# Rounding and subtracting two heads of queries and keys at once, with transfers inside SBUF, in the setups of a decoder layer's two attentions

## The chip, the core and the metric

The kernel runs on one core of a Trainium2 chip. The core has a matrix engine (TensorE, PE in the profile; its weight loads are PEld), a vector engine (VectorE, DVE), a scalar engine (ScalarE, ACT), a general engine (GpSimd, POOL) and a sync engine (SyncE, SP) that issues transfers. Every engine works through its own instructions in the order in which they were built; semaphores make one wait for another. Data lives in SBUF (128 partitions) and in PSUM, which TensorE writes; transfers between HBM and SBUF, or from one place in SBUF to another, run on 16 DMA engines that all queues share. The metric is device time in microseconds from start to end of one execution.

## What is computed

One layer of a hybrid decoder, for a prompt of 1024 tokens and for 8 single-token samples with 8192 cached tokens each. The parts that matter here are the prompt's forgetting attention, 8 heads of 64 columns:

```
def mixer_inputs(xn, w_in, b_f, g_sgu_v):
    h = xn @ w_in
    q = h[..., O_Q:O_K].reshape(B, T, ATT_HEADS, ATT_HEAD_DIM)
    k = h[..., O_K:O_V].reshape(B, T, ATT_HEADS, ATT_HEAD_DIM)
    ...
def fox_attend(q, k, v, cq, ck, qpos, kpos):
    s = einsum('bqhd,bkhd->bhqk', q, k) * ATT_HEAD_DIM ** -0.5
    s = s + (cq[..., :, None] - ck[..., None, :])
    s = where(kpos <= qpos, s, -inf)
    p = softmax(s, axis=-1)
    return einsum('bhqk,bkhd->bqhd', p, v)
```

Around it stand the input projection, a spatial gating unit, an output projection, a cross-attention into 256 memory tokens, a gated MLP with a causal convolution, and for the samples the same layer with attention over a paged cache of keys and values. All inputs and outputs are float32.

## The kernel before

Matrix products of the prompt are made in three parts from operands that are split in two: a high part h, the value rounded to the matrix format fp32r, and a low part l, the value minus h. The prompt runs in one order of stages: input projection, first attention (rows 0 to 511, `hf` 0), second attention (rows 512 to 1023, `hf` 1), then output projection, cross-attention and MLP for each half. The sample work (gathers of cached keys and values, VectorE multiplications and reductions over keys, lines 1427 and 1428 in the attentions, TensorE products over values, line 1488) is laid between at a rate that is set by hand for each stage. The order on each engine is fixed when the kernel is built, by a list scheduler with its own picture of durations; SP and GpSimd issue their transfers in that order too, and an issue that waits holds up what stands behind it.

An attention runs over four head pairs (`hp`), each of two heads (`j`), two blocks of queries (`blk`) and two query tiles (`ii`). Each score tile is two products: the operand `qq[:, 0]` with `ka`, and `qq[0:68, 1]` with `kb` (lines 807 and 809). By partitions:

- `qq[0:64, 0]` and `qq[0:64, 1]` both hold the head's high queries, `qq[64:128, 0]` its low queries, `qq[64:68, 1]` four rows of cumulated gates;
- `ka[0:64]` and `ka[64:128]` both hold the high keys, `kb[0:64]` the low keys, `kb[64:68]` four more gate rows.

So high by high and low by high come from the first product (contracted over 128 partitions), high by low and the gates from the second (over 68).

`setup(hp)` makes these operands in two steps. `load` has fetched the two heads' queries `qn` (one buffer), keys `kn` and values `vn` with tokens on partitions. Step one transposes the queries on TensorE into one PSUM tile `tr` (line 750), whose partitions 0 to 63 are head 0 and 64 to 127 head 1. Then, for each head, ScalarE rounds 64 partitions into `qq[0:64, 0]` (757), GpSimd copies them to `qq[0:64, 1]` (758), and VectorE subtracts into `qq[64:128, 0]` (774). Step two does the same for the keys (transposes 779; 784, 785, 788). In the first attention the prepared keys are stored to `ks_d` (791, 792), and in the second one loaded from there for the first 512 tokens (769, 770). `calm` orders ScalarE's part behind the newest exponential.

The setup of the next head pair is started while the present one is half done: step one after the first block, step two one score tile later. The very first setup is called early, at the end of the input projection, ahead of that projection's last group of matmuls; the second attention's first setup begins in the first attention's last head pair. Between a setup and its first score stand the current pair's last scores, exponentials (813 to 817), transposes of probabilities ("turns", 836, evacuated by 841 and 843) and value products (852, 861, 872). During the first attention, matmuls that prepare the cross-attention's memory (lines 272 to 274, loads of `w_ck` and `w_cv` on SP by line 249) and the spatial gating (631 to 679) are laid between. During the second attention PSUM's four single banks of the pool `ba` become two pairs, so that a score tile of up to 1024 columns has one pair, and the setups' `tr` takes half a pair.

Of the pools, `U` has 18 tiles of 4 KB a partition, `T2` has 7 of 2 KB, the raw weights `wr` 4, and the gathered cache rows `kv` 4. Each is used in turn, and a tile is waited for until what it held has been read.

Of the kernel before, what the change touches and what calls it, by code (L numbers as in the profile page):

```python
# [7 lines left out]
F32 = mybir.dt.float32  # L8
F32R = mybir.dt.float32r
BF16 = mybir.dt.bfloat16  # L10
I32 = mybir.dt.int32
AF = mybir.ActivationFunctionType
ALU = mybir.AluOpType
# [65 lines left out]
def build(nc, tc, ctx, a, phases=None):  # L79
# [27 lines left out]
    def nm(s):  # L107
        cnt[0] += 1
        return f"{s}_{cnt[0]}"

    def U(shape, dt=F32):
        n = 1
        for s in shape[1:]:
            n *= s
        t = upool.tile([P, UW], dt, tag="u", bufs=NU, name=nm("u"))[:, :n]
        if len(shape) == 3:
            t = t.rearrange("p (a b) -> p a b", b=shape[2])
        return t

    def T2(n=512, dt=F32):  # L120
        return tpool.tile([P, 512], dt, tag="t2", bufs=NT, name=nm("t2"))[:, :n]
# [88 lines left out]
    ks_d = dram.tile([NH, 64, 2, 512], F32, tag="ks_d", name="ks_d")  # L210
# [515 lines left out]
    def attention(hf, late=None, at=3):  # L726
# [3 lines left out]
        def load(hp):  # L730
# [9 lines left out]
            nc.sync.dma_start(vn, v_d[: nk * P, cs].rearrange("(i p) c -> p i c", p=P))  # L740
            return qn, kn, vn

        def setup(hp, qn, kn, vn):


            calm = lambda: tc.issue_after(lastexp[0]) if lastexp else nullcontext()
            with behind(ENG.PE):
                tr = (MS, BB, BA)[SB]()
                for i in range(4):
                    nc.tensor.transpose(tr[:, i * P : (i + 1) * P], qn[:, i, :], ident)  # L750
            qab, ka, kb = [], [], []
            for j in range(2):
                h = hp * 2 + j
                rows = slice(64 * j, 64 * j + 64)
                qq = U([P, 2, 512], F32R)
                with calm():
                    nc.scalar.activation(qq[0:64, 0, :], tr[rows, :], AF.Copy)
                nc.gpsimd.tensor_copy(qq[0:64, 1, :], qq[0:64, 0, :].bitcast(F32))
                nc.gpsimd.dma_start(qq[64:68, 1, :], cq_d[h, :, hf * 512 : (hf + 1) * 512])
                qab.append(qq)  # L760
                if hf == 0:
                    kab = U([P, 2, 512], F32R)
                    ka.append(kab[:, 0, :])
                    kb.append(kab[:, 1, :])
                else:
                    ka.append(U([P, nk * P], F32R))
                    kb.append(U([P, nk * P], F32R))
                    for r in range(2):
                        nc.sync.dma_start(ka[j][64 * r : 64 * r + 64, 0:512].bitcast(F32), ks_d[h, :, 0, :])
                    nc.sync.dma_start(kb[j][0:64, 0:512].bitcast(F32), ks_d[h, :, 1, :])  # L770
                nc.gpsimd.dma_start(kb[j][64:68, :], ck_d[h, :, : nk * P])
            for j, qq in enumerate(qab):
                rows = slice(64 * j, 64 * j + 64)
                nc.vector.tensor_tensor(qq[64:128, 0, :], tr[rows, :], qq[0:64, 0, :].bitcast(F32), op=ALU.subtract)
            yield
            with behind(ENG.PE):
                tr = (MS, BB, BA)[SB]()
                for i in range(4):
                    nc.tensor.transpose(tr[:, i * P : (i + 1) * P], kn[:, i, :], ident)
            s = slice(hf * 512, hf * 512 + 512)  # L780
            for j in range(2):
                rows = slice(64 * j, 64 * j + 64)
                with calm():
                    nc.scalar.activation(ka[j][0:64, s], tr[rows, :], AF.Copy)
                nc.gpsimd.tensor_copy(ka[j][64:128, s], ka[j][0:64, s].bitcast(F32))
            for j in range(2):
                rows = slice(64 * j, 64 * j + 64)
                nc.vector.tensor_tensor(kb[j][0:64, s], tr[rows, :], ka[j][0:64, s].bitcast(F32), op=ALU.subtract)
            if hf == 0:
                for j in range(2):  # L790
                    nc.gpsimd.dma_start(ks_d[hp * 2 + j, :, 0, :], ka[j][0:64, :].bitcast(F32))
                    nc.gpsimd.dma_start(ks_d[hp * 2 + j, :, 1, :], kb[j][0:64, :].bitcast(F32))
            got.append((qab, ka, kb, vn))

        def scores(qkv, ls, blk, j, ii):
# [90 lines left out]

        got = []
        first = setup(0, *load(0))
        if hf:
            next(first)  # L890
# [5 lines left out]
        for hp in range(4):  # L896
# [5 lines left out]
            for blk in range(2):  # L902
# [6 lines left out]
                for j in range(2):  # L909
                    for ii in range(2):  # L910
                        p_ = scores(qkv, ls, blk, j, ii)
                        if ii == 0:
                            pt.append(
                                [
                                    (U([P, 4, 256]) if nkt - g > 2 else T2(512).rearrange("p (a b) -> p a b", b=256))
                                    for g in range(0, nkt, 4)
                                ]
                            )
                        queue.append(partial(turn, p_, pt[j], nkt - 1 + ii, ii))
                        if j == 1 and ii == 1:  # L920

                            def fin(*args):
                                r = values(*args)
                                queue.insert(min(BKQ, len(queue)), partial(back, *r))

                            queue.append(partial(fin, qkv, ls, pt, hp, blk))
                        drain(LA[hf])
                        yield 1.8
                        if hp < 3 and (blk, j, ii) == LD[hf]:
                            raw = load(hp + 1)  # L930
                        if hp < 3 and (blk, j, ii) == ST[hf]:
                            nxt = setup(hp + 1, *raw)
                        if nxt:
                            next(nxt, None)
                            yield 1
# [425 lines left out]
    def behind(e):  # L1361

        return tc.issue_after(last[e]) if e in last else nullcontext()
# [480 lines left out]
    def prompt():  # L1844
# [4 lines left out]

        got, ahead = [], []  # L1850
        att1 = attention(1, lambda: got.append(merge_in(0)))
        att0, fill0 = attention(0, (lambda: next(att1)) if LT < 4 else None, LT), fill()

        def early():
# [170 lines left out]
```

## Time and profile before

| what | us |
|---|---|
| runs of the kernel before | 1807.2, 1799.28, 1805.22; median 1805.22 |
| the profiled execution's own time | 1804.14 |
| its span, first to last instruction | 1802.1 |

A profile's group line reads: source line, engine, operation, what is written and what is read by the program's tile names (numbers left out), their shapes and types, how often, then busy time in us and the mean ns of one, then the idle time of that engine just ahead of these instructions and what ended it. A line of the waits reads: the engine and line that waited, what it waited for, then total us, how many waits, the longest. A line of the timeline reads: start in us, duration in us, engine and line, and in brackets an idle time ahead of it with its releaser. Engines marked with a q (SPq, ACTq) are their instruction queues, where transfers are issued.

### The profile page before, as it was taken

What the parts mean: (1) busy time and instruction counts of PE and PEld (TensorE: products, weight loads), DVE (VectorE), ACT (ScalarE), POOL (GpSimd) and SP (SyncE); (2) the same over time, 40 slices, a digit from 0 to 9 for tenths busy, and PEclk for the clock granted to TensorE, in tenths of its full rate; (3) what the DMA queues carried; (4) which work ended last, traced back from release to release, by engine and by line L of the source; (5) the groups of instructions that cost most, each with busy time, mean ns of one, the idle gap of its engine ahead of it and who ended that gap; (6) DMA issues with size and microseconds to landing.
All of it is one profiled execution on the core that took longest, in us unless ns stands there. A gap on an engine that the chain in (4) does not pass through costs nothing.

```text
span 1802.1 us, 25097 instructions
## 1 busy us (share of the span) xinstructions
PE 1737.0 (96%) x9637; PEld 1287.2 (71%) x9637; DVE 1398.2 (78%) x1729; ACT 736.4 (41%) x1378; POOL 506.6 (28%) x461
## 2 busy tenths in 40 slices
PE   8999999878999999999999999999989999999997
PEld 5887777555677667777777777776666778767875
DVE  4689658988788986999999999887875549855344
ACT  6332265465643635333333244336353323332332
POOL 1252333433123332332322223343422112002110
PEclk9999999999999999999999999999999999999999
DMA  8886888786697985778788778988879687568982
GB/s 296 301 298 226 300 317 329 265 273 212 223 407 277 355 331 217 290 291 341 296 305 309 290 302 321 377 304 325 308 276 338 224 297 249 185 260 299 357 312 82
DMA packets 157074, 521.06 MB, mean 289 GB/s; under 512 B 20874, under 2 KB 40842, under 8 KB 124186
## 3 DMA queue, kind: packets, MB, share of 16 engines
q0 software_dynamic: 57168, 341.14, 49.8%
q1 hardware_dynamic: 92874, 165.73, 26.7%
q10 hardware_dynamic: 6912, 12.59, 1.9%
q8 instruction: 76, 1.25, 0.3%
q14 instruction: 44, 0.36, 0.1%
HBM read 495.47 MB, written 23.93 MB: 288 GB/s over the span
## 4 chain that ended last, share of the span: by engine, by line
PE 47%; DMA 11%; issue 8%; DVE 6%; POOL 2%; ACT 1%; POOLq 0%; DVEq 0%
DMA kv<-cache_v,io 7%; PE ba L272 6%; PE ba L274 6%; PE ba L273 6%; PE dv L1488 3%; PE bb L272 3%; PE bb L274 3%; PE bb L273 3%; DMA kv<-cache_k,io 2%; DVE s L1440 2%; DVE kv L1436 1%; PE dv L331 1%; PE dv L1764 1%; POOL kv L1482 1%; POOL kv L1420 1%
## 5 line engine op out<-in xcount | busy, mean ns | idle before, releaser
L235 ACT ACTIVATE wh<-wr 128x1024 fp32r<-128x1024 f32 (+2 forms) x220 | 228.9, 1044 | 421.5 <-PE ba L273 138.8
L236 DVE TENSOR_TENSOR wl<-wr,wh 128x1024 fp32r<-128x1024 f32 (+2 forms) x220 | 262.9, 1199 | 172.6 <-PE ba L274 57.7
L1420 POOL DMA_INDIRECT kv<-cache_k,io x128 | 199.2, 1556 | 570.9 <-DVE s L1440 325.3
L1436 DVE TENSOR_TENSOR kv<-kv,d 128x1024 f32<-128x1024 f32 (+1 forms) x156 | 258.1, 1681 | 24.7 <-DMA kv<-cache_k,io 24.7
L1440 DVE TENSOR_REDUCE s<-kv 128x16 f32<-128x1024 f32 (+1 forms) x156 | 258.1, 1672 | 0.0
L1482 POOL DMA_INDIRECT kv<-cache_v,io x128 | 168.5, 1317 | 254.9 <-PE dv L1488 177.5
L272 PE MATMUL ba<-u,wh 128*128 128x512 f32 x528 | 209.3, 397 | 0.0
L273 PE MATMUL ba<-u,wh 128*128 128x512 f32 x528 | 208.8, 396 | 0.5 <-DVE u L239 0.5
L274 PE MATMUL ba<-u,wl 128*128 128x512 f32 x528 | 208.8, 396 | 0.0
L272 PE MATMUL ba<-wh,u 128*128 128x512 f32 (+1 forms) x495 | 186.4, 379 | 2.6 <-ACT u L235 2.6
L273 PE MATMUL ba<-wl,u 128*128 128x512 f32 (+1 forms) x495 | 185.1, 375 | 1.2 <-DVE wl L236 1.2
L274 PE MATMUL ba<-wh,u 128*128 128x512 f32 (+1 forms) x495 | 183.2, 375 | 0.0
L1488 PE MATMUL dv<-kv,s 128*32 128x512 f32 x1024 | 127.7, 606 | 3.6 <-DMA kv<-cache_v,io 3.5
L272 PEld LDWEIGHTS ba<-u,wh 128*128 128x128 f32 x528 | 99.5, 188 | 27.2 <-issue 5.6
L274 PEld LDWEIGHTS ba<-u,wl 128*128 128x128 f32 x528 | 99.3, 188 | 26.5 <-issue 4.0
L273 PEld LDWEIGHTS ba<-u,wh 128*128 128x128 f32 x528 | 99.3, 188 | 25.8 <-issue 3.1
L272 PEld LDWEIGHTS ba<-wh,u 128*128 128x128 f32 x495 | 93.0, 188 | 27.0 <-issue 6.5
L272 PE MATMUL bb<-u,wh 128*128 128x512 f32 x272 | 108.7, 400 | 0.0
L274 PE MATMUL bb<-u,wl 128*128 128x512 f32 x272 | 107.8, 397 | 0.0
L273 PE MATMUL bb<-u,wh 128*128 128x512 f32 x272 | 107.6, 396 | 0.0
L273 PEld LDWEIGHTS ba<-wl,u 128*128 128x128 f32 x495 | 93.0, 188 | 20.0 <-DVE wl L236 1.9
L274 PEld LDWEIGHTS ba<-wh,u 128*128 128x128 f32 x495 | 92.9, 188 | 19.5 <-issue 1.6
(445 smaller groups left out, 3313.8 us busy)
## 6 DMA issues: line engine op xcount, KB each, us to landing
wr<-w_up SPq DMA_DIRECT2D x88, 512.0 KB
kv<-w_up POOLq DMA_DIRECT2D x22, 1024.0 KB, 7.6
wr<-w_down SPq DMA_DIRECT2D x40, 512.0 KB
kv<-w_down POOLq DMA_DIRECT2D x11, 1024.0 KB, 8.3
wr<-w_in SPq DMA_DIRECT2D x16, 512.0 KB
wr<-w_o SPq DMA_DIRECT2D x16, 512.0 KB
wr<-w_cq SPq DMA_DIRECT2D x16, 512.0 KB
wr<-w_co SPq DMA_DIRECT2D x16, 512.0 KB
```

What stands on the lines that cost most here:

```text
L235: nc.scalar.activation(h, src, AF.Copy)
L236: nc.vector.tensor_tensor(l, src, h.bitcast(F32), op=ALU.subtract)
L272: mmul(out, sh, mh, start=(i == 0), stop=False)
L273: mmul(out, sh, ml, start=False, stop=False)
L274: mmul(out, sl, mh, start=False, stop=(i == n - 1))
L331: mmul(ps[32 * j : 32 * j + 32, :w], xT[:, k, :] if nk == 8 else xT[:, k * 8 : k * 8 + 32], raw[:, q, j * w : (j + 1) * w], start=(k == 0) ...
L1420: nc.gpsimd.indirect_dma_start(kv, None, a["cache_k"], off(kidx[:, b, ch : ch + 1]))
L1436: nc.vector.tensor_tensor(kvv[:, i : i + m, :], kvv[:, i : i + m, :], qb.unsqueeze(1).broadcast_to((P, m, 512)), op=ALU.mult)
L1440: nc.vector.tensor_reduce(s[:, ch * 4 + i : ch * 4 + i + m, :].rearrange("p k h -> p (k h)"), kvv[:, i : i + m, :].rearrange("p k (h d) -> ...
L1482: nc.gpsimd.indirect_dma_start(kv, None, a["cache_v"], off(kidx[:, b, ch : ch + 1]))
L1488: mmul(dv[32 * j : 32 * j + 32, :], s[:, ch * 4 : ch * 4 + 4, :].rearrange("p k h -> p (k h)"), kvv[:, j, :], start=(ch == 1), stop=(ch == ...
L1764: mmul(ps[32 * j : 32 * j + 32, :P], xsT[:, k, :], rvs[j // 2][:, k, j % 2, :], start=(k == 0), stop=(k == 7), tile_position=(0, 32 * j),)
```

## The change

A new helper `halves` rounds all 128 partitions of `tr` with one ScalarE instruction and subtracts them with one on VectorE. The high part is written over the tile that was transposed (`qn` or `kn`), the low part into a new `T2` tile. Each operand part, 64 partitions of 512 columns, is then brought to its place by a transfer from SBUF to SBUF that SP issues: for each head three for the queries and three for the keys, twelve a setup. GpSimd's copies are gone, and the store of prepared keys becomes two transfers of 128 partitions instead of four of 64, still on GpSimd's queue.

```
+        def halves(tr, rows_, calm):
+            h = rows_.rearrange("p i c -> p (i c)")
+            with calm():
+                nc.scalar.activation(h.bitcast(F32R), tr, AF.Copy)
+            l = T2(512, F32R)
+            nc.vector.tensor_tensor(l, tr, h, op=ALU.subtract)
+            return h, l.bitcast(F32)
...
+            qh, ql = halves(tr, qn, calm)
             for j in range(2):
                 h = hp * 2 + j
                 rows = slice(64 * j, 64 * j + 64)
                 qq = U([P, 2, 512], F32R)
-                with calm():
-                    nc.scalar.activation(qq[0:64, 0, :], tr[rows, :], AF.Copy)
-                nc.gpsimd.tensor_copy(qq[0:64, 1, :], qq[0:64, 0, :].bitcast(F32))
+                for dst, part in ((qq[0:64, 0, :], qh), (qq[0:64, 1, :], qh), (qq[64:128, 0, :], ql)):
+                    nc.sync.dma_start(dst.bitcast(F32), part[rows, :])
...
-            for j, qq in enumerate(qab):
-                rows = slice(64 * j, 64 * j + 64)
-                nc.vector.tensor_tensor(qq[64:128, 0, :], tr[rows, :], qq[0:64, 0, :].bitcast(F32), op=ALU.subtract)
             yield
...
+            kh, kl = halves(tr, kn, calm)
             for j in range(2):
                 rows = slice(64 * j, 64 * j + 64)
-                with calm():
-                    nc.scalar.activation(ka[j][0:64, s], tr[rows, :], AF.Copy)
-                nc.gpsimd.tensor_copy(ka[j][64:128, s], ka[j][0:64, s].bitcast(F32))
-            for j in range(2):
-                rows = slice(64 * j, 64 * j + 64)
-                nc.vector.tensor_tensor(kb[j][0:64, s], tr[rows, :], ka[j][0:64, s].bitcast(F32), op=ALU.subtract)
+                for dst, part in ((ka[j][0:64, s], kh), (ka[j][64:128, s], kh), (kb[j][0:64, s], kl)):
+                    nc.sync.dma_start(dst.bitcast(F32), part[rows, :])
             if hf == 0:
-                for j in range(2):
-                    nc.gpsimd.dma_start(ks_d[hp * 2 + j, :, 0, :], ka[j][0:64, :].bitcast(F32))
-                    nc.gpsimd.dma_start(ks_d[hp * 2 + j, :, 1, :], kb[j][0:64, :].bitcast(F32))
+                for r, part in ((0, kh), (1, kl)):
+                    nc.gpsimd.dma_start(ks_d[hp * 2 : hp * 2 + 2, :, r, :].rearrange("h p n -> (h p) n"), part)
```

## The prediction

> **What bounds the kernel now.** I read the page's busy times first, then the span cut into stages.
>
> ```profile
> PE 1737.0 (96%) x9637; PEld 1287.2 (71%) x9637; DVE 1398.2 (78%) x1729; ACT 736.4 (41%) x1378; POOL 506.6 (28%) x461
> ```
> ```profile
> 239.00:310.00 71.00, 70.84 (x364) 54.20 (x363) 50.42 (x81) 45.07 (x91) 26.12 (x35) 1.00 0.85 314
> 310.00:480.00 170.00, 143.46 (x974) 101.25 (x972) 146.96 (x265) 99.39 (x227) 56.04 (x76) 0.98 0.73 239
> 480.00:1802.00 1322.00, 1292.54 (x7079) 953.20 (x7076) 1029.32 (x1218) 502.40 (x928) 354.28 (x298) 0.99 0.79 294
> ```
> (Columns: stretch, its length, busy PE, PEld, DVE, ACT, POOL with counts, clock, DMA share, GB/s.) The whole kernel is bound by TensorE. The eight setups lie between 239 and 455 us. Until 310 TensorE has weight matmuls between the scores and idles 0.2 us of 71, so a faster setup is worth nothing there. From 310 to 480 it idles 170 - 143.5 = 26.5 us, and VectorE is busy 86%: this is the one stage in which the change can win. What is won or lost there shifts all that follows, because after 480 TensorE is again busy 98%.
>
> The waits of that stage say who is late.
>
> ```profile
> ACT t L814 <- DVE mx L813: 14.3, 8, 5.6
> ACT wr L817 <- DVE mx L816: 13.5, 13, 3.0
> DVE mx L816 <- PE ba L811: 9.9, 6, 3.2
> PE ba L807 <- ACT wr L817: 6.8, 6, 1.9
> POOL kv L1420 <- DVE s L1428: 34.2, 7, 9.5
> ```
> The loop is score (L807), maximum on VectorE (L816), exponential on ScalarE (L817), next score. ScalarE waits 27.8 us for maxima, more than VectorE waits for scores: VectorE's queue is mostly the late one. GpSimd's gathers wait for buffers, not behind the setups' casts.
>
> **What is removed.** The subtractions and roundings of two heads become one each.
>
> ```profile
> L236 DVE TENSOR_TENSOR u<-ba,u 128x512 fp32r<-128x512 f32 x10 | 6.8, 676 | 2.3 <-ACT u L235 2.3
> L774 DVE TENSOR_TENSOR u<-ba,u 64x512 fp32r<-64x512 f32 x16 | 11.0, 689 | 1.3 <-ACT u L843 1.0
> L788 DVE TENSOR_TENSOR u<-ba,u 64x512 fp32r<-64x512 f32 x16 | 11.0, 685 | 3.2 <-ACT u L784 1.5 <-issue 1.5
> L235 ACT ACTIVATE u<-ba 128x512 fp32r<-128x512 f32 x10 | 5.9, 594 | 8.1 <-PE ba L1208 8.1
> L757 ACT ACTIVATE u<-ba 64x512 fp32r<-64x512 f32 x16 | 9.4, 589 | 0.2
> ```
> ```profile
> 310.00:371.00 61.00, 4.13 (x6) 1.00 0.84 279
> 371.00:480.00 109.00, 4.13 (x6) 0.97 0.67 217
> ```
> The same subtraction on 128 rows (L236, PSUM to SBUF) takes 676 ns, no more than 64 rows take, so each setup keeps two of its four: 32 of 11.0 + 11.0 us become 16, 11 us less on VectorE. The last two rows are L774 alone: 12 of its 16 instructions lie from 310 on, so the stage loses half of 24 subtractions, 12 x 0.687 = 8.2 us. Of this I let 0.6 shorten the stage, 4.9 us: at most 0.86 could, VectorE's busy share, and about a third is the floor that I would believe, since head pairs in which VectorE waits for scores gain nothing. ScalarE likewise saves 12 x 0.59 = 7.1 us there, but it is busy 58% and waits for VectorE; I take nothing. The transposes' PSUM bank is read for two instructions and not four; that helps only beyond what VectorE gives, so nothing again.
>
> GpSimd loses its 32 casts and half of the 16 stores of keys (eight of twice the size stay).
>
> ```profile
> L758 POOL CAST u<-u x16: 599/629/1707, 240.5 to 451.2; 64x512 fp32r<-64x512 f32 x16
> L785 POOL CAST u<-u x16: 604/609/717, 243.0 to 453.7; 64x512 fp32r<-64x512 f32 x16
> L1427 DVE TENSOR_TENSOR kv<-kv,d x64: 656/681/1052, 269.0 to 499.4; 128x512 f32<-128x512 f32 x64
> ```
> (Minimum, median, maximum.) That is 16 x 0.629 + 16 x 0.609 = 19.8 us of an engine busy a third of the stage, whose gathers wait for buffers: nothing. The medians lie within 30 ns of the minima on either engine, so the casts hardly slow VectorE's multiplications. [...]
>
> **What is added.** Per setup twelve SP transfers of 128 KB inside SBUF. No row shows one. The nearest are loads of the same size on SP for the issue, and stores of the same size from SBUF, on GpSimd's queue, for the landing.
>
> ```profile
> L770 SPq DMA_DIRECT2D u<-ks_d x8: 472/538/705, 356.9 to 443.2; - x8
> ...
> L792 POOL DMA_DIRECT2D ks_d<-u x8: 521/522/569, 247.3 to 354.8; - x8
> ...
> DMA to landing us min/median/max: 2.3/3.9/8.5
> ```
> So 0.54 us to issue and 2.3 to 8.5 us to land; I take the stores' median, 3.9. Issue comes to 12 x 0.54 = 6.5 us of SP per setup, in order. [...]
>
> In traffic it is 96 x 0.131 = 12.6 MB, 9.4 MB of it (six setups) in the stage.
>
> ```profile
> q1 hardware_dynamic: 16528, 15.73, 31.6%
> ```
> SP's queue moves 15.73 MB in 31.6% of 170 us, 293 GB/s, so 9.4 MB are 32 us of all engines: the share rises from 0.73 to 0.92. It fits, but can lengthen landings.
>
> Who waits for the new transfers? Room is the time from the end of the first head's subtraction (half of the pair shown) to the head pair's first score.
>
> ```profile
> 325.19 1.40 DVE L788 TENSOR_TENSOR u<-ba,u 64x512 fp32r<-64x512 f32 x2
> 353.10 1.39 DVE L788 TENSOR_TENSOR u<-ba,u 64x512 fp32r<-64x512 f32 x2
> 366.12 1.40 DVE L788 TENSOR_TENSOR u<-ba,u 64x512 fp32r<-64x512 f32 x2
> 453.28 1.39 DVE L788 TENSOR_TENSOR u<-ba,u 64x512 fp32r<-64x512 f32 x2 [1.45 <-issue]
> ```
> ```profile
> 328.08 0.31 PE L807 MATMUL ba<-u,u 128*128 128x128 f32 x1
> ...
> 354.38 0.60 PE L750 MATMUL ba<-cp,qn 128*128 128x128 f32 x4
> 354.73 0.31 PE L807 MATMUL ba<-u,u 128*128 128x128 f32 x1
> ...
> 356.43 0.63 PE L836 MATMUL bb<-cp,t 128*128 128x128 f32 x4 [0.26 <-ACT u L843]
> ...
> 360.91 1.73 PE L852 MATMUL ms<-u,u 128*64 128x256 f32 x14
> ...
> 371.15 0.39 PE L807 MATMUL ba<-u,u 128*128 128x320 f32 x1
> ...
> 459.58 0.39 PE L807 MATMUL ba<-u,u 128*128 128x320 f32 x1
> ```
> A key's low half now needs 0.54 + 3.9 = 4.4 us after its subtraction. Second attention: 371.15 - 366.82 = 4.3 us of room in head pair 0 and 459.58 - 453.97 = 5.6 in head pair 3, enough within 0.1 us. First attention, head pair 2: 328.08 - 325.89 = 2.2, but the built order puts 24 weight matmuls ahead of this score, which at 70.84 us / 364 of the first stage take 4.7: covered. Head pair 3 has 354.73 - 353.79 = 0.9, and the built order moves four turns (L836, 0.63) and a values group (L852, 1.73) ahead of it: 3.3 us of room against 4.4.
>
> At this same place lies the worst wait. The second attention's first queries are transposed just ahead of that score (354.38), and their load has moved on SP.
>
> ```profile
> 345.94 0.37 SPq L733 DMA_DIRECT2D qn<-q_d  x1
> ```
> It was issued right behind the previous transposes. Now qn is the transfers' own source, has one buffer, and its load stands behind all twelve transfers. The last three of these follow the low half of the keys, ready at about 353.2 (353.10 + 0.69, less the subtraction saved ahead of it): SP is free at 353.2 + 3 x 0.54 = 354.8, and the load lands 3.9 us later, at 358.7. TensorE comes there at 354.38 + 2.36 of moved work = 356.7. It stalls 2.0 us, and the scores, transposes and gather matmuls queued behind it wait with it. This stall contains the 1.1 us of the key. With a landing of 2.3 us it is 0.4, with 8.5 it is 6.6.
>
> First setup: SP carries twelve transfers (6.5 us) ahead of the memory rows and the third weight of w_ck.
>
> ```profile
> 246.46 0.38 SPq L249 DMA_DIRECT2D wr<-w_ck  x1
> ```
> ```profile
> 259.52 1.06 ACT L235 ACTIVATE wh<-wr 128x1024 fp32r<-128x1024 f32 x1 [2.24 <-DMA wr<-w_ck]
> ```
> That weight goes out near 250 instead of 246.5, and ScalarE, which now waits 2.24 us for the fourth, would round that one later by the 1 us or so that SP is behind by then. TensorE is on the input projection's last matmuls meanwhile (it idles 0.2 us in this stretch), so I put it at nothing, 1 us if that cover is gone. Next keys, values and gating rows, also behind the transfers now, are read a whole head pair later.
>
> Sum against the profiled execution's 1804.1 us: - 4.9 + 2.0 = 1801.2. The runs' median, 1805.2, is 1.1 above that execution, one third of which I allow for: 1801.5.
>
> **The rivals.**
> 1. *Operands come late, slower.* SP's queue and fuller DMA engines bring landings of 8.5 us, that row's maximum, in every setup. Then 6.6 us at 355, 9.0 - 4.3 = 4.7 in head pair 0, 9.0 - 5.6 = 3.4 in head pair 3, and 9.0 - 2.2 - 4.7 = 2.1 in the first attention's pair 2: 17 us, less the gain 1816. For it: the transfers come in bursts, and the slice in which the first attention's third setup falls has the DMA engines full already (the share is the last number but one):
>
> ```profile
> 310.00:330.00 20.00, 16.22 (x102) 11.35 (x100) 19.81 (x31) 8.39 (x18) 8.59 (x11) 1.00 1.00 328
> ```
> Against: those stores queue behind gathers, SP's transfers do not. It decides from a landing of about 5.2 us, where stalls reach the 4.9 gained.
> 2. *More is freed.* All of VectorE's 11.0 us counts, or the casts had cost VectorE time: 1804.1 - 11 = 1793. For it: VectorE at 86% in the stage. Against: the idle that it spends behind scores.
> 3. *Nothing changes.* VectorE's saved time turns into waiting for L811, as 9.9 us do now, and the transfers are hidden: 1804. The change then does what it says, on an engine that does not set the end.
>
> **How the numbers follow.** My forecast 0.40, late operands 0.30, more freed 0.15, nothing 0.14, the rest 0.01 slower. A difference under 0.5%, 9 us, is about what a measurement of this kernel cannot tell from no change. Forecast: 0.37 within it, 0.03 beyond on the fast side; nothing: within; late operands: 0.21 over 9 us, 0.09 within; more freed: faster. So faster 0.18, same 0.60, slower 0.22. The range goes from 1793 (rival 2) to 1817 (rival 1); my own case alone gives 1797 to 1804.
>
> **What would show it.** Right: line 767's and 791's transfers about 0.54 us each on SP; 16 subtractions fewer; VectorE's busy time from 310 to 480 down by some 8 us and TensorE's idle there down by 2 to 4; a wait of TensorE at line 750 for qn near 355. Wrong: scores (lines 809 and 811 of the changed kernel) waiting for transfers in several head pairs, gathers landing late, or a stage as long as before with VectorE idler.

## The result, and the profile after

The changed kernel takes 1853.11 us (median of six runs, 1849.50 to 1859.67), the kernel before beside it 1802.16 (six runs, 1797.95 to 1807.20). The ratio is 1.0282, 95% interval 1.0261 to 1.0303: 51 us slower. The prediction, 1801.5 with a range to 1817, was wrong, and on the wrong side.

The profiled execution took 1849.5 us, its span is 1847.7. First the page's line of busy times, then the same stretches as before the change, then from the first setup to the last value product of the second attention (239 to 544), and the rest.

```profile
PE 1756.5 (95%) x9637; PEld 1296.4 (70%) x9637; DVE 1385.6 (75%) x1713; ACT 725.4 (39%) x1362; POOL 459.7 (25%) x421
```
```profile
239.00:310.00 71.00, 62.85 (x300) 45.19 (x298) 43.13 (x70) 37.52 (x76) 15.12 (x18) 0.93 0.98 312
310.00:480.00 170.00, 126.30 (x741) 87.94 (x739) 109.44 (x207) 70.71 (x171) 38.12 (x47) 0.86 0.86 258
...
239.00:544.00 305.00, 247.19 (x1439) 171.76 (x1438) 192.47 (x343) 142.96 (x319) 63.65 (x77) 0.89 0.86 265
544.00:1848.00 1304.00, 1278.63 (x6971) 945.20 (x6969) 1020.76 (x1204) 492.55 (x911) 330.38 (x293) 0.99 0.79 294
```

The same work in the kernel before ended at 492; its two stretches in the same view:

```profile
239.00:492.00 253.00, 226.09 (x1432) 163.44 (x1430) 206.07 (x359) 153.51 (x335) 84.97 (x114) 0.99 0.77 262
492.00:1802.00 1310.00, 1280.75 (x6982) 945.21 (x6980) 1020.64 (x1204) 493.34 (x910) 351.47 (x295) 0.99 0.79 294
```

All of the loss lies in the stage of the eight setups, which grew from 253 to 305 us; the rest is 6 us shorter. VectorE is busy 13.6 us less in the stage and GpSimd 21, so the engines did lose the work that the change takes away. TensorE does practically as many instructions in it (1439 and 1432 in these counts) but idles 57.8 us instead of 26.9, and is busy 21.1 us longer at the same work, since its clock fell from 0.99 to 0.89. So of the stage's 52 us, 31 are waiting and 21 are the clock that followed.

Who is waited for? TensorE's waits in the stage of the changed kernel:

```profile
PE ba L809 <- DMA u<-t: 13.0, 3, 6.1
PE ba L809 <- ACT wr L819: 7.9, 4, 5.8
PE bb L838 <- ACT wr L819: 5.6, 4, 2.4
PE ms L854 <- ACT u L845: 3.9, 4, 2.3
...
PE ba L811 <- DMA u<-t: 3.1, 3, 1.7
...
PE ba L811 <- DMA u<-ks_d: 2.8, 2, 2.2
...
PE ba L809 <- DMA u<-ks_d: 1.9, 2, 1.7
```

Scores (809, 811) wait for transfers in several head pairs, which the prediction had named as the sign against it. SyncE's queue shows why, in its own lines and its waits:

```profile
L767 SPq DMA_DIRECT2D u<-qn x32: 467/588/1590, 239.8 to 497.3; - x32
...
L791 SPq DMA_DIRECT2D u<-t x32: 461/478/1028, 246.3 to 510.8; - x32
```
```profile
SPq L791 <- DMA u<-qn: 13.6, 10, 4.2
...
SPq L767 <- DMA qn<-q_d: 12.3, 4, 7.7
...
SPq L791 <- DMA u<-ks_d: 6.6, 5, 2.2
SPq L740 <- DMA u<-t: 6.2, 3, 2.7
```

An issue costs some 0.5 to 0.6 us, as predicted. But many issues first wait until an earlier transfer has landed (in this trace the 554 transfers of SyncE and ScalarE carry eight completion semaphores, mostly in rotation; in all 503 cases in which it has the whole landing of the transfer before on the same semaphore, the next issue on it started only after that landing, in 75 of them within 0.2 us). One setup of the second attention, the third, as the timeline has it:

```profile
453.05 1.11 SPq L767 DMA_DIRECT2D u<-qn  x2
...
458.19 0.69 DVE L749 TENSOR_TENSOR t<-ba,t 128x512 fp32r<-128x512 f32 x1 [0.20 <-ACT t L747]
...
464.84 0.44 SPq L779 DMA_DIRECT2D u<-ks_d  x1
467.53 3.72 SPq L791 DMA_DIRECT2D u<-t  x3
467.72 0.39 PE L809 MATMUL ba<-u,u 128*128 128x320 f32 x1 [1.72 <-DMA u<-ks_d]
473.08 1.74 SPq L791 DMA_DIRECT2D u<-t  x3
474.92 0.53 SPq L733 DMA_DIRECT2D qn<-q_d  x1
...
480.27 0.93 PE L809 MATMUL ba<-u,u 128*128 128x320 f32 x2 [5.50 <-DMA u<-t]
```

The low half of the keys is ready at 458.88, but SyncE is still at the queries' six transfers and the six reloads of prepared keys: seven of these twelve are out, the eighth is being issued. The keys' first transfer goes out 8.7 us later, the last ends its issue at 474.8, and only then is the next pair's query load issued. The 18 issues took from 453.1 to 474.8, 1.2 us each. The pair's first score, at 467.72, needs only the reloaded half of the keys, and it waits for that: the reload stands among the queries' transfers. The next stall, 5.50 us at 480.27, is for the keys' own transfers.

How long a transfer of SyncE took to land can be read from the trace too, from the last rise of its completion semaphore before that semaphore's next use. Over the eight setups the medians are 7.1 and 9.8 us for the queries' high and low pieces (line 767), and 8.1 and 9.1 us for the keys' (line 791, its 32 transfers `u<-t` and its 16 `u<-u`), with 2.2 the shortest and 15.5 the longest. With eight semaphores, landings of 8 us let one issue out every 1.0 us (an estimate, 8 us divided by eight), however little an issue itself costs. One setup was spared, the last of the first attention, with landings of 2.2 to 3.9 us; in the setup shown, those issued from 456 on took 8.0 to 14.3. The two stretches:

```profile
366.00:379.00 13.00, 8.81 (x60) 5.49 (x58) 11.43 (x28) 7.57 (x22) 3.81 (x5) 1.00 0.81 215
456.00:483.00 27.00, 16.71 (x93) 11.03 (x93) 14.24 (x23) 8.76 (x17) 4.49 (x7) 0.77 1.02 267
```

The DMA engines (last number but one, their busy share) are busy 0.81 in the first and 1.02 in the second. In these two stretches the long landings go with the fuller DMA engines; that the one makes the other was not shown, no run tests it.

### The profile page after: what moved, and what is told of

It is laid out like the page before. It is cut to its first block, busy times and chain, and to the rows that moved or that the text cites. A ratio compares the mean times of both kernels' runs of the same rounds, so it can differ in the third digit from the quotient of the medians.

```text
span 1847.7 us, 25197 instructions
## 1 busy us (share of the span) xinstructions
PE 1756.5 (95%) x9637; PEld 1296.4 (70%) x9637; DVE 1385.6 (75%) x1713; ACT 725.4 (39%) x1362; POOL 459.7 (25%) x421
## 4 chain that ended last, share of the span: by engine, by line
PE 58%; DMA 17%; issue 11%; DVE 9%; POOL 3%; ACT 2%; SPq 0%; POOLq 0%; ACTq 0%; DVEq 0%
PE ba L272 8%; PE ba L274 7%; PE ba L273 7%; DMA kv<-cache_v,io 5%; PE dv L1490 4%; PE bb L272 4%; PE bb L274 4%; PE bb L273 4%; DVE kv L1438 2%; DMA kv<-cache_k,io 2%; DVE s L1442 2%; DMA u<-t 2%; DMA wr<-w_in 2%; DMA u<-ks_d 1%; DMA u<-u 1%
## 5 line engine op out<-in xcount | busy, mean ns | idle before, releaser
L1422 POOL DMA_INDIRECT kv<-cache_k,io x128 | 181.6, 1419 | 601.5 <-DVE s L1442 344.6
L1484 POOL DMA_INDIRECT kv<-cache_v,io x128 | 164.2, 1283 | 321.1 <-PE dv L1490 221.6
```

Source lines behind the costliest of these rows:

```text
L1422: nc.gpsimd.indirect_dma_start(kv, None, a["cache_k"], off(kidx[:, b, ch : ch + 1]))
L1484: nc.gpsimd.indirect_dma_start(kv, None, a["cache_v"], off(kidx[:, b, ch : ch + 1]))
```

## The experiments

Every ratio is to the kernel before, run on the same chip beside it; "over" is the ratio less one, times 1802 us. A caution holds for all of them: each edit also moves some instructions in the built order, and two edits below that add about as much work to the engines (7 and 9) differ by 10 us. So a few us between two edits say little, even where the interval is narrower.

The theories at the start: (1) SyncE's queue, which issues in order and waits for landings, makes the operands late (1a) or the loads behind the transfers (1b); (2) 12.6 MB more are too much for the DMA engines; (3) halves made at once cost by themselves, through tiles held longer or the order of the instructions. Later H is the holding of tiles until transfers have landed, L late operands, Q the queue, S ScalarE's own stores.

**1. The same halves, carried by GpSimd.** Both transfer lines become a copy.

```
-                    nc.sync.dma_start(dst.bitcast(F32), part[rows, :])
+                    nc.gpsimd.tensor_copy(dst, part[rows, :])
```

> The halves of both heads are still made at once, but GpSimd copies each of the twelve pieces of a setup to its operand; SyncE has no transfer between SBUF places left. Theory 1, the transfers' way through SyncE's queue costs the 51 us (in-order issue, each behind the landing of an earlier one): 1795 to 1810 us, since 16 subtractions and 16 roundings are still saved. Theory 2, the 12.6 MB more on the DMA engines cost them: the same 1795 to 1810. Theory 3, making the halves at once is itself the cost (the transposes' copy and the small tiles are held longer, the order of the instructions moves): 1840 to 1855, as with the transfers.

1842.5 us, 1.0239 (1.0206 to 1.0273), 43 over. As theory 3 said, but its trace names another cause, in the waits of GpSimd and TensorE:

```profile
POOL u L791 <- DMA kv<-cache_k,io: 28.1, 6, 5.8
POOL u L767 <- DMA kv<-cache_v,io: 19.8, 3, 7.4
POOL u L767 <- DMA kv<-cache_k,io: 17.4, 4, 6.1
...
PE ba L811 <- POOL u L791: 8.9, 4, 3.8
```

The copies stand in GpSimd's queue until gathers of cache rows have landed, and scores wait for the copies. The run does not tell halves made at once from pieces carried in order; run 9 does.

**2. The transfers on GpSimd's queue.** `nc.sync.dma_start` becomes `nc.gpsimd.dma_start` in the same two lines.

> The changed kernel with the same twelve transfers of a setup issued by GpSimd instead of SyncE: the same bytes, the same SBUF places. Theory 1, SyncE's queue: loads of weights, queries, values and memory rows no longer stand behind transfers, so most of the loss goes, 1803 to 1825 us; what is left over 1802 is the scores' wait for landings of 4 to 6 us. Theory 2, bytes on the DMA engines: nothing gets better, 1845 to 1860. Theory 3, halves at once: 1840 to 1855.

1846.7 us, 1.0244 (1.0220 to 1.0267), 44 over. That SyncE's other loads suffer is thus not needed for a loss of this size: they are free of transfers here. But the transfers now share a queue with the gathers, so the run does not show what those loads cost in the change itself. On GpSimd's queue the trace shows landings (line 791's transfers, minimum, median, maximum):

```profile
DMA to landing us min/median/max: 2.2/7.8/9.7
```

**3. Transfers that nobody reads.** The kernel before, and behind its subtractions twelve transfers of its operands to DRAM on SyncE.

```
+                for c, part in enumerate((qq[0:64, 0, :], qq[0:64, 1, :], qq[64:128, 0, :])):
+                    nc.sync.dma_start(xs_d[hf, hp, 0, j, c], part.bitcast(F32))
...
+                for c, part in enumerate((ka[j][0:64, s], ka[j][64:128, s], kb[j][0:64, s])):
+                    nc.sync.dma_start(xs_d[hf, hp, 1, j, c], part.bitcast(F32))
```

> The kernel before, operands made by the engines as before, and behind each setup's operands twelve transfers of 128 KB of them on SyncE, to places in DRAM that nothing reads. Theory 1, if it is the loads held up behind the transfers on SyncE: 1820 to 1850 us, most of the loss without any score waiting for a transfer. Theory 1 in its other form, the scores waiting for their own operands: 1802 to 1810. Theory 2, the bytes: 1840 to 1860. Theory 3, halves at once: 1802 to 1810.

1815.8 us, 1.0075 (1.0055 to 1.0096), 14 over. Between the forecasts: more than where only operands or halves count (to 1810), less than where held-up loads or bytes carry the loss (from 1820). Transfers on SyncE are a cost even when nobody waits for them, about a quarter of the loss. ScalarE's waits show one way in which it is paid, weights of the cross-attention that come late:

```profile
ACT wh L236 <- DMA wr<-w_cv: 15.0, 5, 8.2
```

In the kernel before, the same wait is 0.3 us in all.

**4. The change in the second attention alone.**

```
+        setup = setup_n if hf == 1 else setup_
```

> The change in the second attention alone (hf 1), the first attention's setups as before. In the changed kernel the first scores of head pairs lag 27 us behind when the second attention begins and 46 us when its last pair begins. If the loss is local to each setup, the second attention brings 19 of 46 parts of 51 us: 1818 to 1828 us. Theory 2, by bytes: half the 12.6 MB, 1822 to 1832. If the first attention's late start is what makes the second lose (weights and memory rows late, transfers meeting them), 1802 to 1810.

1833.9 us, 1.0188 (1.0159 to 1.0217), 34 over. Above the forecast of a local loss (to 1828) and far above that of a loss handed on from the first attention: the second attention alone is enough for two thirds of it. The first alone was not run.

**5. Scores that do not wait for their setup.** All transfers stay, but pairs 1 to 3 read pair 0's operands; and the same edit in the kernel before as a control.

```
             qkv, nxt = got.pop(), None
+            held0 = qkv[:3] if hp == 0 else held0
+            qkv = (*held0, qkv[3])
```

> The changed kernel, every instruction and every transfer of its setups kept, but the scores of head pairs 1 to 3 of each attention read the operands of head pair 0, so no score of these pairs waits for its own setup; the operands made for them are not read. Theory 1a, late operands (the detour through a transfer delays the first score of each pair): the loss falls to that of unread transfers on the same queue, 1808 to 1822 us. Theory 1b, SyncE's other loads stand behind the transfers: 1835 to 1855. Theory 3, the halves' tiles are held too long (the queries' rows are source of the transfers and have one buffer, the small tiles too), which delays the next setups: 1835 to 1855, too.

> Control: the kernel before with the same reading of head pair 0's operands by the scores of pairs 1 to 3. If scores hardly wait for their setups there, 1796 to 1806 us; what it gains over 1802 has to be taken off the gain of the changed kernel with the same edit.

1846.7 us, 1.0233 (1.0198 to 1.0268), 42 over; the control 1800.9, 0.9988 (0.9973 to 1.0004). Theory 1a falls as the whole cause: without the waits of six of the eight pairs 42 of 51 us are still lost. TensorE's waits in the same stretch show what took their place:

```profile
PE ms L854 <- ACT u L845: 11.3, 5, 7.2
PE ba L809 <- ACT wr L819: 8.7, 6, 5.7
PE bb L838 <- ACT wr L819: 7.5, 2, 5.1
PE ba L809 <- DMA u<-ks_d: 7.3, 1, 7.3
```

The 16.1 us for `u<-t` are gone from TensorE's list. Of these the longest, 6.07 us at 397.9, was head pair 0's own: that score began 0.1 us after a reload's landing (397.8), and here the same score waits 7.3 us for `ks_d`, which the edit leaves. In the other pairs 18.1 us of TensorE's waits for SyncE's transfers went, and the kernel gained 9. The waits for ScalarE have grown (line 854's from 3.9 to 11.3), and ScalarE itself still stands 18.8 us until SyncE's transfers have landed (7.4 for `u<-t`, 7.1 for `u<-u`, 4.3 for `u<-qn`). Waiting for an operand was the wait that ended last, with others close behind it.

**6. The keys alone, the queries alone.** In each, one of the two calls of `halves` with its transfers is taken back to the code before, for the keys alone so:

```
-            qh, ql = halves(tr, qn, calm)
...
-                for dst, part in ((qq[0:64, 0, :], qh), (qq[0:64, 1, :], qh), (qq[64:128, 0, :], ql)):
-                    nc.sync.dma_start(dst.bitcast(F32), part[rows, :])
+                with calm():
+                    nc.scalar.activation(qq[0:64, 0, :], tr[rows, :], AF.Copy)
+                nc.gpsimd.tensor_copy(qq[0:64, 1, :], qq[0:64, 0, :].bitcast(F32))
...
+                nc.vector.tensor_tensor(qq[64:128, 0, :], tr[rows, :], qq[0:64, 0, :].bitcast(F32), op=ALU.subtract)
```

> The change for the keys alone (6 transfers a setup, 2 subtractions and 2 roundings become 1 each); the queries' operands made as before. Theory 1a, late operands: the keys are made last, nearest to the first score, so they carry most of the loss, 1825 to 1842 us. Theory 1b or the bytes: half of each, 1822 to 1832. Theory 3 by the queries' rows: little, 1803 to 1815.

> The change for the queries alone; the keys' operands made as before. Theory 1a, late operands: the queries have a step of the loop more until the first score, so 1803 to 1818 us. Theory 1b or the bytes: half the loss, 1822 to 1832. Theory 3 by the queries' rows, held by the transfers while the next load of them waits: most of it, 1830 to 1850.

Keys 1823.6 us, 1.0119 (1.0088 to 1.0150), 21 over; queries 1818.5, 1.0090 (1.0057 to 1.0122), 16 over. No part carries most of it.

**7. Tiles held by transfers.** Halves at once on top of the kernel before, and the unread transfers take these as their source.

```
+            qh, ql = halves(tr, qn, calm)
...
+                for c, part in enumerate((qh, qh, ql)):
+                    nc.sync.dma_start(xs_d[hf, hp, 0, j, c], part[rows, :])
```

> The kernel before with the halves of both heads made at once on top of its own operands (two roundings and two subtractions of 128 rows more in each setup), and the twelve transfers of a setup reading these halves and going to places in DRAM that nothing reads. So the queries' rows, the keys' rows and the small tile of the low half are held until transfers land, as in the changed kernel, but no score waits for a transfer. Theory H, tiles held by the transfers delay the next setups and exponentials: 1835 to 1855 us. Theory L and Q, only late operands and the queue: 1816 to 1828 (the 1816 of the earlier unread transfers and some of the 4 instructions' 8 x 2.5 = 20 us).

And the same halves read by nothing, without any transfer:

> The kernel before with the halves of both heads made at once on top of its own operands and read by nothing: two roundings and two subtractions of 128 rows more in each setup, no transfer. It splits the 30 us of the unread transfers from such halves. Theory H, tiles held until transfers land: these instructions alone cost 3 to 8 us (16 subtractions are 11 us of VectorE, half of that on the path), 1804 to 1810, and holding the rest. If the instructions themselves are what costs: 1812 to 1820.

1831.2 us, 1.0164 (1.0125 to 1.0203), 30 over, and 1812.3, 1.0057 (1.0038 to 1.0076), 10 over. With the 14 of run 3, 6 of the 30 are left for holding the tiles, which the widths of the three intervals cannot tell from nothing. A try from the other side, more buffers for the halves, stays without an answer: the room had to come from the gathers' buffers, and that alone costs far more than was in question.

```
-NKV = 4
+NKV = 3
...
-            l = T2(512, F32R)
+            l = tpool.tile([P, 512], F32R, tag="lo", bufs=2, name=nm("lo"))
...
-            qn = tpool.tile([P, 512], F32, tag="qn", bufs=1, name=nm("qn")).rearrange("p (i c) -> p i c", c=P)
+            qn = tpool.tile([P, 512], F32, tag="qn", bufs=2, name=nm("qn")).rearrange("p (i c) -> p i c", c=P)
```

> Control for the next: the changed kernel with three instead of four buffers for gathered cache rows, which frees 8 KB a partition and can cost something by itself. 1850 to 1880 us; no theory is tested.

> The changed kernel with three buffers for gathered cache rows, as in the control, and the room spent on the halves: two buffers of their own for the low halves, and two instead of one for the queries' rows. Theory H, tiles held by transfers: 15 to 35 us below the control. Theory L and Q: within 8 us of the control.

1977.9 us and 1979.7. The extra buffers bring nothing there, but in a kernel that by then waits for gathers.

**8. ScalarE's own stores.** In the changed kernel's timeline ScalarE stops twice ahead of a store of the memory's keys, for the landing of SyncE's transfers (a third such stop, 3.59 us, follows at 341):

```profile
290.50 0.34 ACTq L721 DMA_DIRECT2D o_mk<-t  x1
290.89 0.49 ACT L845 ACTIVATE u<-bb 128x384 f32<-128x384 f32 x1 [4.25 <-DMA u<-qn]
...
303.24 0.34 ACTq L721 DMA_DIRECT2D o_mk<-t  x1
303.63 0.60 ACT L845 ACTIVATE u<-ms 128x512 f32<-128x512 f32 x1 [7.33 <-DMA u<-u]
```

Line 721 was given to GpSimd (`nc.scalar` to `nc.gpsimd`).

> The changed kernel with the stores of the memory's keys and values (line 721) issued by GpSimd instead of ScalarE. In the changed kernel's trace ScalarE sat 4.25, 7.33 and 3.59 us in front of what follows three of these stores until transfers of SyncE had landed. Theory S, ScalarE's own stores wait for SyncE's transfers and hold up the exponentials behind them: 1832 to 1845 us. If these waits lie beside others as late: 1848 to 1858.

1848.6 us, 1.0273 (1.0237 to 1.0308), 49 over, not to be told from the change itself: 15 us of waits removed from an engine, and next to nothing gained. The stops are real, but they lay beside others as late.

**9. No operand carried by a transfer.** Halves at once, brought to the operands by the engines that made them before.

```
-                    nc.sync.dma_start(dst.bitcast(F32), part[rows, :])
+                nc.scalar.activation(qq[0:64, 0, :], qh[rows, :], AF.Copy)
+                nc.gpsimd.tensor_copy(qq[0:64, 1, :], qq[0:64, 0, :].bitcast(F32))
+                nc.vector.tensor_copy(qq[64:128, 0, :], ql[rows, :])
```

(the keys likewise)

> The halves of both heads made at once as in the change, and brought to the operands by the engines that made the operands before: ScalarE copies the high halves, GpSimd their duplicates, VectorE the low halves; no transfer on any queue. Against the kernel before: two instructions of ScalarE and two of VectorE more in each setup, and a longer way from the transposes to the operands. If making halves at once costs by itself (order of the instructions, small tiles): 1830 to 1850 us, as with GpSimd's copies. If the loss needs a queue that carries twelve pieces in order (SyncE's or GpSimd's): 1804 to 1818.

1801.6 us, 1.0001 (0.9989 to 1.0012): no change. This run tells the carrying from the halves. Halves made at once and their longer way cost nothing measurable, although this kernel even does two instructions of ScalarE and two of VectorE more in a setup than before. So the loss is in how the pieces are carried: by transfers, or all by GpSimd behind its gathers. Theory 3 falls, but for tiles that are held by transfers in flight.

**10. What the saved work is worth.** The kernel before, with the second head's roundings and subtractions left out.

```
-                with calm():
+                if j == 0:
+                    with calm():
...
-            for j, qq in enumerate(qab):
+            for j, qq in enumerate(qab[:1]):
...
-                mmul(s, qab[j][:, 0, i * P : (i + 1) * P], ka[j][:, ch * n : ch * n + n], start=True, stop=False)
+                mmul(s, qab[0][:, 0, i * P : (i + 1) * P], ka[0][:, ch * n : ch * n + n], start=True, stop=False)
```

> The kernel before with 16 roundings and 16 subtractions fewer, as many as the change saves, and no transfer: operands are made for the first head of each pair alone, and both heads' scores read them (the second head's own scores are left out). This is what the saved work is worth by itself. The prediction's step (4.9 us, 60 per cent of VectorE's 8.2 in the stage): 1793 to 1800 us. All of VectorE's 11.0: 1789 to 1793. If it is worth nothing: 1800 to 1806.

1799.3 us, 0.9981 (0.9969 to 0.9993): 3.4 us gained, interval 1.3 to 5.6.

**11. How the loss goes with the number of pieces.** Eight transfers a setup, GpSimd copying the duplicates; then all twelve, the keys' six on GpSimd's queue.

```
-                for dst, part in ((qq[0:64, 0, :], qh), (qq[0:64, 1, :], qh), (qq[64:128, 0, :], ql)):
+                for dst, part in ((qq[0:64, 0, :], qh), (qq[64:128, 0, :], ql)):
                     nc.sync.dma_start(dst.bitcast(F32), part[rows, :])
+                nc.gpsimd.tensor_copy(qq[0:64, 1, :], qh[rows, :])
```

> The changed kernel with eight transfers a setup instead of twelve: the duplicates of the high halves are copied by GpSimd, four a setup, as many casts as before the change. If the loss goes with the number of transfers that SyncE issues in order (18 with the keys' reload in the second attention, now 14): a third of 51 us less, 1832 to 1842. If each transfer's landing matters and not their number: 1845 to 1856.

> The changed kernel with the queries' six transfers of a setup on SyncE as they are and the keys' six on GpSimd's queue: the same twelve transfers and bytes, but no queue carries more than six pieces in order (twelve on SyncE with the reload of the keys). If the loss comes from one queue's pieces in order, the keys' behind the queries': 1818 to 1832 us, near the kernels with six transfers (1818 and 1824). If it adds up over transfers wherever they are: 1838 to 1842 (16 + 21 us). If the bytes on the DMA engines decide: 1845 to 1856.

Eight: 1831.8 us, 1.0154 (1.0126 to 1.0182), 28 over, at the fast edge of the forecast by number (the bytes fall by the same third, so this does not part the two). Two queues: 1.0215 (1.0167 to 1.0263), 39 over. That is the sum of keys alone and queries alone, 37, and less than 51 by an amount that the intervals hardly hold apart. All twelve on GpSimd's queue (run 2) had cost 44.

**12. Number or bytes.** The unread transfers of run 3, with 32 of 512 columns each.

```
-                    nc.sync.dma_start(xs_d[hf, hp, 0, j, c], part.bitcast(F32))
+                    nc.sync.dma_start(xs_d[hf, hp, 0, j, c, :, 0:32], part[:, 0:32].bitcast(F32))
```

> The unread transfers on SyncE again (1816 us), behind the operands of the kernel before, with as many transfers but 32 of 512 columns in each: 0.8 MB instead of 12.6. If their bytes on the DMA engines cost the 14 us: 1801 to 1806. If it is their number, issued in order on SyncE: 1812 to 1818.

1809.7 us, 1.0035 (1.0018 to 1.0052), 6 over. Between the two forecasts: of the 14 us about half go with the number of transfers, half with the bytes. Whether the number costs by SyncE's issues or on the DMA engines, the run does not tell.

## Why the prediction was wrong

**The gain was right.** 4.9 us were forecast for the saved arithmetic, 3.4 (1.3 to 5.6) measured without transfers. VectorE lost 13.6 us of busy time in the stage, for the 11.0 worked out over all setups. Rival 2, all of VectorE's time, falls with it. Its other ground, that GpSimd's casts had cost VectorE time, can be read from VectorE's multiplications of the changed kernel, which has no casts in its setups:

```profile
L1429 DVE TENSOR_TENSOR kv<-kv,d x64: 656/682/693, 266.9 to 547.5; 128x512 f32<-128x512 f32 x64
```

Their maximum fell from 1052 to 693 ns, their median stayed (681 to 682), and all 64 took 42.9 us before and 42.5 after: 0.4 us less is all that these instructions show of the casts' removal.

**The issue price was right, the worst place nearly.** Median issues of 0.48 to 0.59 us, for 0.54. The stall for the second attention's first queries came where it was forecast, 1.6 us for 2.0:

```profile
378.97 0.66 PE L759 MATMUL ba<-cp,qn 128*128 128x128 f32 x4 [1.60 <-DMA qn<-q_d]
```

**The step that failed** is "Who waits for the new transfers?", and in it the sentence "A key's low half now needs 0.54 + 3.9 = 4.4 us after its subtraction". The eight setups took 12.7, 16.8, 9.8, 3.7, 15.9, 17.0, 21.9 and 17.2 us from the end of the keys' subtraction to the landing of the first head's low half, where rooms of 3.3 to 6.9 us had been compared with 4.4. Both terms failed. The landing was taken as 3.9 us; its medians on SyncE were 7.1 to 9.8. And SyncE was taken as free when the keys' halves are ready, while in the setup shown the keys' first transfer went out 8.7 us later. The price of an issue is not to blame for that: twelve issues at 0.54 are 6.5 us, and in the second attention of the kernel before 7.4 us or more lie between the queries' first rounding and the end of the first head's keys' subtraction. They took 12.2 us (453.05 to 465.28) because issues waited for landings, for which the prediction had no term. By its own 3.9 us there would be no such wait, since eight issues at 0.54 take 4.3. So the long landings cost twice, once by themselves and once through the queue. The one setup in which 4.4 us held, at 3.7, is the last of the first attention, where the prediction had looked for the worst wait.

A row that spoke against 3.9 was at hand in the kernel before: the eight stores beside those of L792, of the same size and on the same queue.

```profile
L791 POOL DMA_DIRECT2D ks_d<-u x8: 537/564/602, 243.5 to 352.3; - x8
...
DMA to landing us min/median/max: 3.1/5.6/6.8
```

Their median lies beyond the 5.2 us from which, by the prediction's own sum, stalls eat the gain.

**Terms put at nothing.** "Next keys, values and gating rows" behind the transfers were put at nothing, the memory's rows and weights at nothing or 1 us. Transfers that nobody reads cost 14 us, about 6 for their number and 7 for their bytes; ScalarE's 15.0 us of waits for w_cv in that run show one way. The cover that was counted on until 310 gave way too: TensorE idles 8.1 us in that stretch, for 0.2 before. "It fits, but can lengthen landings", said of the traffic, was half of that and had no term.

**No term for the clock.** 21 of the 52 us that the stage grew are TensorE's slower clock. The sum added stalls one by one and never asked what a stall does to the work behind it.

**The rivals.** Rival 1, late operands, had the mechanism nearest to the truth: its landing of 8.5 us is close to the medians, and its 17 us of stalls, added up over four pairs, to the 26 us that TensorE waited for SyncE's transfers (13.0 + 3.1 + 2.8 + 1.9 in the list above, 1.6 for the queries' load, 3.6 at 299.6 for a piece of the keys). It still missed the time by some 37 us, because it had nothing for the other engines that wait and for the clock. The argument against it, that GpSimd's stores stand behind gathers and SyncE's transfers do not, did not help: SyncE's landings were as long as those on GpSimd's queue. Taking the operands' waits away in six of eight pairs gave back 9 of 51 us, 2 of which the control gains too. What the runs do show: the carrying is the cause (0 when three engines copy the pieces), it grows with the pieces and their bytes together (16 and 21 for six, 28 for eight, 39 to 51 for twelve), and it comes with SyncE's queue and with GpSimd's.

**Open.** Of the 51 us (54 with the gain that was paid back), 14 were measured by themselves, as transfers on SyncE that nobody waits for. The other 40 are not divided among operands that come late, tiles held until a transfer has landed, and engines that stop ahead of their own transfers: with one of them removed, the others took its place each time. A run with two of them removed at once was not made. A kernel with more completion semaphores, or with less other load on the DMA engines, was not run.

## What to carry to other kernels

When small transfers are added to a queue, ask how long they take to land while the DMA engines are as full as they will be there (here some 8 us, for 3.9 assumed), and whether an issue has to wait for an earlier landing; then add up all that this queue must issue between two dependent steps, loads that were already there included, and compare that with the room. The price of an issue alone (0.54 us) says little. A copy that an engine makes on its way (a write from PSUM to the place where it is needed) can be cheaper than a wider instruction with transfers behind it: here 16 subtractions and 16 roundings were worth 3.4 us, while the twelve transfers a setup behind them cost 54. Where several engines wait in a ring, removing the wait that a profile names need not give its time back; look at what is late next before pricing it.

## What the runs showed of the hardware

TensorE's granted clock fell after stalls, eight times in the changed kernel's stage, and stayed low for 3.4 to 13.7 us each time. Around the stall of 6.07 us at 397.9 and the next of 5.80 at 410, four windows of 10 us, and one of 13 further on:

```profile
381.00:391.00 10.00, 8.88 (x67) 5.42 (x66) 7.44 (x17) 7.74 (x26) 3.62 (x5) 1.00 1.04 316
391.00:401.00 10.00, 3.93 (x18) 2.48 (x18) 0.17 (x2) 1.85 (x5) 0.00 (x0) 0.72 1.00 273
401.00:411.00 10.00, 3.73 (x19) 2.57 (x16) 5.00 (x11) 3.14 (x8) 1.04 (x1) 0.67 0.81 244
411.00:421.00 10.00, 10.00 (x61) 7.94 (x62) 9.10 (x16) 6.04 (x14) 3.14 (x5) 0.76 0.45 141
...
433.00:446.00 13.00, 10.74 (x42) 6.53 (x44) 7.48 (x13) 4.62 (x10) 1.52 (x2) 0.50 1.03 315
```

The third column is TensorE's busy time, the last but two the clock: in the fourth window it is busy throughout, and the clock is still 0.76 on average. The trace's records of the clock hold two values alone, 1.0 and 0.5. The 0.5 lasts 65 us of the changed kernel's stage, in pieces of 3.4 to 13.7 us, and 7 us of the stage before. In the 3.4 us ahead of each of the eight drops, as long as the shortest piece, TensorE was busy for 0 to 1.8 us. The values products' matmuls of 128x256 in the stage took 379 ns at 1.0 and 634 at 0.5 (medians of 187 and 60). In this stage the slower clock added two thirds to the waiting itself (21 us beside 31).

Landings of 128 KB inside SBUF, on GpSimd's queue, had medians of 6.9 us (line 767, from 2.2 to 10.3) and 7.8 us (line 791, above), three times the lowest and more. On SyncE's queue in the changed kernel the medians were 7.1 to 9.8 us, from 2.2 to 15.5. From a setup's first issue to its last landing (11 to 29 us) the DMA engines were busy 0.79 in the setup whose landings took 2.2 to 3.9 us, and 0.95 to 1.04 in the other seven.
